# Residual sums of two MLPs run on in PSUM by ScalarE's copies; one product moves to another bank; squares are written in the transposes' order; the transposing transfers are issued on ScalarE's queue

## The chip, the cores and the metric

One core of a Trainium2 chip. TensorE (PE) multiplies, VectorE (DVE) and ScalarE (ACT) work elementwise, GpSimd (POOL) does little here, and SyncE (SP) issues DMA transfers; ACT can issue them too. Each engine works through its own list of instructions in order. The metric is the time of one execution in microseconds of the device.

## The reference

A trunk of two layers over 256 frames of width 2048, all in fp32. Each layer normalizes, mixes (layer 0 by stick-breaking attention, layer 1 by a top-64 sparse attention), adds to the residual `x`, and then runs an MLP, which is where this change lies:

```python
for i in range(DEPTH):                      # DEPTH = 2
    h = rms_norm(x, norm_mix[i])
    x = x + mixer(h)                        # one of two kinds
    h = rms_norm(x, norm_mlp[i])
    x = x + jnp.square(jax.nn.relu(h @ w_up[i])) @ w_down[i]   # 2048 -> 8192 -> 2048
```

## The kernel before

**Products.** An fp32 product is made of parts. Each weight tile is copied by ACT to a rounded first half `wh` (`copy`, L104), DVE subtracts to get the second half `wl` (L1002), and TensorE multiplies: the left operand's two parts with `wh`, its first part with `wl`. An item is one such weight tile: 12 matmuls of 128x512 for a tile of `w_down`, 6 for a tile of the products below. The function `load` (L968) issues the weight loads on SP's queue, `high` makes `wh` four items ahead, `low` makes `wl` three items ahead. There are five buffers for `wh` and four for `wl`.

**Blocks.** The MLP's hidden width of 8192 is worked in eight blocks f of 1024. Block 0 goes the plain way. Blocks 1 to 7 compute their part of `h @ w_up` by seven products of half the size instead of eight (`seven`), with sums of weights (`two`, `other`, `three`, `last_sum`: L406, L410, L415, L418) and sums of results. The first 16 items of a block accumulate P1 and another product in the two banks of one PSUM tile (`pair`, named acc) and two products in single banks (`v`, `z`, named aux). After them `between` copies P1 from the pair into SBUF (`se(0)`) and `between2` and later `after` and `after2` form the sums on DVE (L445 to L456). The last 12 items use the bank `y` for P2 and the pair again. `after` adds P1 and P2 on DVE (L451).

**From results to the hidden tile.** `square_up` applies Relu and Square on ACT. For blocks 1 to 6 the result must be turned so that tokens lie along the free axis: DVE transposes 32x32 pieces (`squares`, L473, reading 16 bytes apart), SP writes each half n of the tile to DRAM (`away`, L482, tile hd) and reads it back in another order (`back`, four transfers per half, L488); ACT and DVE then split it into the two parts of the hidden tile hS (`parted_h`, L494 and L495). Half 1 goes first, half 0 a little later. Block 7 is turned on TensorE (`turn`).

**Down.** `down(f)` multiplies hS with `w_down` in four groups of 512 columns, four items each, half 1 of hS first. A group accumulates in one of three PSUM tiles of two banks (acc). At its end `down_done` has DVE compute `xs = acc * rs2 + xs` for both token halves (L262; L532 for the last block of the last layer, in pieces of 256 columns, followed by the output transfers). `rs2` undoes the normalization, which is put off to here.

**Order.** The items of block f's products are spread among the down items of blocks f-2 and f-1, 28 + 16 items per block. The steps after the products are hung behind items by times in units of TensorE's work (`ends`, `LAPS`). Within these rules a scheduler that belongs to the build sets the order on each engine, except where an instruction is kept in program order (the loads, the transfers to and from DRAM, the splitting into hS).

Of the kernel before, what the change touches and what calls it, by code (L numbers as in the profile page):

```python
# [52 lines left out]
LAG = 2.7  # L53
RAWS = {"wraw": RAW, "sraw": 5}
# [11 lines left out]
class Item:  # L66


    def __init__(self, raws, a, b, mm, moving=False, source=None):
        self.raws, self.a, self.b, self.mm, self.moving, self.post = raws, a, b, mm, moving, []  # L70
        self.source, self.then, self.us = source or (lambda: raws[0].ap), None, 2.72

# [6 lines left out]
def trunk(ctx, tc, x, norm_mix, w_in_a, w_out_a, w_in_b, w_out_b, q_norm_b, k_norm_b, rel_bias,  # L79
# [126 lines left out]
    def tokens_out(items, key, w, r0, c0, lhs, q, done, n=KT, apart=False):  # L206


        def mm(wh, wl):
            if q == 0 and apart:  # L210
                accs[key] = [auxp.tile([P, 512], F32, name="aux") for _ in range(2)]
            elif q == 0:
                acc = accp.tile([P, 2, 512], F32, name="acc")
                accs[key] = [acc[:, t, :] for t in range(2)]
            acc = accs[key]
            for w, parts in ((wh, (0, 1)), (wl, (0,))):
                for t in range(2):
                    for j in range(KB):
                        k = KB * q + j
                        for part in parts:  # L220
                            pin(pe.matmul(acc[t], lhs(k, part, slice(t * P, (t + 1) * P)), w[:, j, :],  # L221
                                          start=w is wh and part == 0 and k == 0,
                                          stop=w is wl and k == n - 1))
        it = plain(rows(w, r0 + KB * P * q, KB * P, c0, 512), KB, 512, mm, True)
        if q == n // KB - 1:
            it.post.append(lambda: done(accs.pop(key)))
# [29 lines left out]
    def add_residual(c, next_col, acc, scale=None):  # L256
        for t in range(2):
            xc = xs[:, t, c * 512:(c + 1) * 512]
            if scale is None:
                dve.tensor_add(xc, acc[t], xc)  # L260
            else:
                dve.scalar_tensor_tensor(xc, acc[t], scale[:, t:t + 1], xc,  # L262
                                         op0=OP.mult, op1=OP.add)
# [15 lines left out]
    def mlp(l, next_col):  # L279
# [6 lines left out]
        def stats():  # L286
# [5 lines left out]
            dve.tensor_mul(sec["rs2"], sec["rs2"], sec["rs2"])  # L292

# [68 lines left out]
        def seven(f, c0):  # L362
# [38 lines left out]
            for s in range(HK // KB):  # L401
# [24 lines left out]
                second += [item([b21], single("y"), quarter(1, 0), s, lambda b=b21: b.ap),  # L426
# [21 lines left out]
            def after():  # L448
                g["s2"] = flat("jc")
                copy(g["s2"], pair(0)())  # L450
                dve.tensor_add(se(0), g["y"], se(0))  # L451
                dve.tensor_sub(se(2), se(2), pair(0)())

            def after2():
                dve.tensor_sub(se(1), se(1), pair(0)())
                dve.tensor_add(g["s2"], pair(1)(), g["s2"])  # L456

            def turn(n, c0, c1):
# [3 lines left out]
                for k in range(4):  # L462
                    for t, c in enumerate((c0, c1)):
                        pe.transpose(ps[:, k, t * P:(t + 1) * P], c[:, k * P:(k + 1) * P], ident)
# [4 lines left out]
            def squares(n, *cs):  # L469

                sq = g["sq", n]
                for t, c in enumerate(cs):
# [600 lines left out]
```

## Time and profile before

| | |
|---|---|
| time, median of 3 runs | 2113.52 us (2111.05 to 2117.68) |
| profiled execution, time and span | 2116.24 us, 2114.5 us |
| granted clock, mean | 0.994 |
| busy: PE, DVE, ACT | 2058.0, 1750.2, 1217.4 us |
| MLP of layer 0 and of layer 1, roughly | 399 to 1103 us, 1415 us to the end |
| residual sums L262: count, each | 120, 0.745 us |
| transposes L473: count, each | 48, 1.07 us |
| ACT's split into hS L494: count, idle before | 24, 39.2 us |

A group row names line, engine, operation, out<-in with shapes and count, then busy us and mean ns of one, then the idle time of the engine just before, and what ended it. In a timeline row the first numbers are the start and the length in us, and the bracket is the idle time before it with the instruction that ended it. SPq and ACTq are the DMA-issuing queues of SP and ACT. The profiled execution stands 2.7 us above the median of the runs shown.

### The profile page before, as it was taken

Reading aid. Unit: us, or ns where it says so; the run is one execution under the profiler, and the core shown is the slowest. Engines: PE = TensorE matmul, PEld = TensorE weight load, DVE = VectorE, ACT = ScalarE, POOL = GpSimd, SP = SyncE. Lnnn points to the kernel's source line nnn. Section 1 sums busy time; section 2 is a strip of 40 time slices with the busy share of each in tenths; the row PEclk is TensorE's granted clock in tenths of the full one; section 3 lists DMA queues with packets and bytes.
Section 4 is the critical chain, followed back from the end, with each engine's and each line's share of the span. In section 5 each row is a group of like instructions: output and inputs, shape, how many; then the busy total and the mean of one; then the engine's idle time right before and its main releaser. Section 6 shows DMA issues by size and latency. Waiting matters only on the chain.

```text
span 2114.5 us, 26501 instructions
## 1 busy us (share of the span) xinstructions
PE 2058.0 (97%) x9572; PEld 1697.1 (80%) x9572; DVE 1750.2 (83%) x1881; ACT 1217.4 (58%) x1560; POOL 34.1 (2%) x71
## 2 busy tenths in 40 slices
PE   8999999999999999999999999999999999999999
PEld 7888888888777787777888788888877778777787
DVE  5456665799999999999865877779999999999985
ACT  6445555665565655665654555666656556555562
POOL 0101110000000000000000000000000000000000
PEclk9999999999999999999999999999999999999999
DMA  7666645755766757677466565465585776757754
GB/s 257 192 184 191 181 161 179 227 191 198 230 203 211 230 192 239 201 226 223 167 195 191 156 195 174 150 208 182 198 258 172 227 228 200 248 189 236 209 180 142
DMA packets 274040, 424.04 MB, mean 201 GB/s; under 512 B 16498, under 2 KB 107252, under 8 KB 273908
## 3 DMA queue, kind: packets, MB, share of 16 engines
q1 hardware_dynamic: 266148, 414.92, 61.6%
q10 hardware_dynamic: 7760, 7.43, 1.2%
q8 instruction: 75, 1.23, 0.2%
q14 instruction: 57, 0.47, 0.1%
HBM read 404.41 MB, written 17.82 MB: 200 GB/s over the span
## 4 chain that ended last, share of the span: by engine, by line
PE 84%; DVE 8%; DMA 4%; SPq 2%; ACT 1%; issue 1%; DVEq 0%; ACTq 0%
PE acc L221 45%; PE acc L242 15%; PE acc L379 12%; PE aux L379 8%; DVE wl L1002 3%; DMA t<-hd 3%; DVE t L473 2%; SPq L488 1%; DVE wraw L406 1%; ACT wh L104 1%; PE aux L160 1%; DVE xs L262 1%; ACT hS L494 1%; DVE sraw L410 1%; PE aux L871 0%
## 5 line engine op out<-in xcount | busy, mean ns | idle before, releaser
L1002 DVE TENSOR_TENSOR wl<-wraw,wh 128x1024 fp32r<-128x1024 f32 x626 | 758.5, 1220 | 224.9 <-PE acc L221 112.0
L104 ACT ACTIVATE wh<-wraw 128x1024 fp32r<-128x1024 f32 x626 | 649.1, 1055 | 455.4 <-PE acc L221 171.2
L221 PE MATMUL acc<-wh,hS 128*128 128x512 f32 x2016 | 516.6, 391 | 23.4 <-ACT hS L494 22.8
L221 PEld LDWEIGHTS acc<-wh,hS 128*128 128x128 f32 x2016 | 377.3, 188 | 108.7 <-ACT hS L494 27.9
L104 ACT ACTIVATE wh<-sraw 128x1024 fp32r<-128x1024 f32 x224 | 233.8, 1055 | 205.4 <-DVE sraw L418 158.0
L1002 DVE TENSOR_TENSOR wl<-sraw,wh 128x1024 fp32r<-128x1024 f32 x224 | 270.7, 1219 | 22.4 <-PE acc L379 11.8
L221 PE MATMUL acc<-wl,hS 128*128 128x512 f32 x1008 | 269.7, 391 | 6.9 <-DVE wl L1002 6.9
L242 PE MATMUL acc<-xT,wh 128*128 128x512 f32 x896 | 230.4, 396 | 0.0
L221 PEld LDWEIGHTS acc<-wl,hS 128*128 128x128 f32 x1008 | 188.3, 188 | 50.4 <-DVE wl L1002 12.0
L242 PEld LDWEIGHTS acc<-xT,wh 128*128 128x128 f32 x896 | 159.8, 188 | 30.1
L221 PE MATMUL acc<-wh,xT 128*128 128x512 f32 x640 | 165.2, 397 | 0.5 <-ACT wh L104 0.5
L379 PE MATMUL aux<-wh,xS 128*128 128x512 f32 x448 | 128.7, 406 | 14.4 <-ACT wh L104 14.4
L221 PEld LDWEIGHTS acc<-wh,xT 128*128 128x128 f32 x640 | 119.6, 190 | 27.5 <-issue 2.3
L221 PE MATMUL acc<-wh,oT 128*128 128x512 f32 x512 | 133.1, 395 | 0.0
L242 PEld LDWEIGHTS acc<-xT,wl 128*128 128x128 f32 x896 | 122.1, 188 | 10.4
L242 PE MATMUL acc<-xT,wl 128*128 128x256 f32 x896 | 126.9, 281 | 0.0
L379 PE MATMUL acc<-wh,xS 128*128 128x512 f32 x448 | 126.1, 397 | 0.6
L379 PE MATMUL acc<-wh,xT 128*128 128x512 f32 x448 | 123.6, 398 | 0.0
L379 PEld LDWEIGHTS aux<-wh,xS 128*128 128x128 f32 x448 | 86.5, 196 | 38.3 <-ACT wh L104 20.4
L221 PEld LDWEIGHTS acc<-wh,oT 128*128 128x128 f32 x512 | 94.7, 188 | 18.9
L379 PEld LDWEIGHTS acc<-wh,xS 128*128 128x128 f32 x448 | 85.0, 192 | 21.9 <-ACT wh L104 4.5
L379 PEld LDWEIGHTS acc<-wh,xT 128*128 128x128 f32 x448 | 86.1, 192 | 18.3
(196 smaller groups left out, 2255.9 us busy)
## 6 DMA issues: line engine op xcount, KB each, us to landing
wraw<-in_w_down_dram SPq DMA_DIRECT2D x256, 512.0 KB, 4.7
sraw<-in_w_up_dram SPq DMA_DIRECT2D x168, 512.0 KB, 4.7
wraw<-in_w_in_a_dram SPq DMA_DIRECT2D x96, 512.0 KB, 3.7
wraw<-in_w_up_dram SPq DMA_DIRECT2D x88, 512.0 KB, 4.1
wraw<-in_w_in_b_dram SPq DMA_DIRECT2D x64, 512.0 KB, 3.7
wraw<-in_w_out_a_dram SPq DMA_DIRECT2D x32, 512.0 KB, 3.5
wraw<-in_w_out_b_dram SPq DMA_DIRECT2D x32, 512.0 KB, 4.0
hd<-t SPq DMA_DIRECT2D x24, 512.0 KB, 6.6
```

The costliest lines, as they stand in the source:

```text
L104: pin(act.activation(o, i, AF.Copy, scale=scale))
L160: pin(pe.transpose(ps[:, j, t * P:(t + 1) * P], block[t][:, ks], ident))
L221: pin(pe.matmul(acc[t], lhs(k, part, slice(t * P, (t + 1) * P)), w[:, j, :], start=w is wh and part == 0 and k == 0, stop=w is wl and k == ...
L242: pe.matmul(acc[:, m, cs], w[:, j, m * P:(m + 1) * P], xT[:, k, xs_, :], start=w is wh and k == 0, stop=w is wl and k == KT - 1)
L262: dve.scalar_tensor_tensor(xc, acc[t], scale[:, t:t + 1], xc, op0=OP.mult, op1=OP.add)
L379: pe.matmul(acc, x(k, part), w[:, j, :], start=opens and w is wh and part == 0 and k == 0, stop=w is wl and k == HK - 1, **on)
L406: dve.tensor_add(b11.ap, b11.ap, b12.ap)
L410: dve.tensor_add(b12.ap, b12.ap, b22.ap)
L473: dve.transpose(sq[:, t].rearrange("p (q k a) -> p q k a", q=4, k=4), c.rearrange("p (q b k) -> p q k b", q=4, k=4))
L488: tc.keep_in_program_order(nc.sync.dma_start(to[32 * q:32 * q + 32], hd[q]))
L494: tc.keep_in_program_order(act.activation(hi, raw, AF.Copy))
L1002: pin(dve.tensor_sub(wl, raw, wh.bitcast(F32)))
```

## The change

**Residual sums.** A down group's PSUM tile is opened six items ahead (`SEED`), and ACT copies the residual `xs` into it (`seeded`; in block 0 multiplied by 1/rs2, which `stats` now also computes). The matmuls of the group all accumulate. At the group's end ACT copies the tile back to `xs` (`down_done`); in the last block ACT and DVE each multiply one token half by rs2 on the way.

**P1 to P2's bank.** `between` copies P1 from the pair into the bank `y`, and P2's matmuls accumulate on top. `after` has ACT apply Relu from that bank; L451 goes.

**Squares and transposes.** `squared` has ACT write the squares in the order in which the transposes read them, into the tile that is later read back; the transposes (`turned`) then read and write without gaps, back into `se`.

**Transfers.** `away` and `back` are issued on ACT's queue, `away` as two transfers of 256 KB per half instead of one of 512 KB. The output transfers of the last block are shared between the queues by token half.

```diff
-    def tokens_out(items, key, w, r0, c0, lhs, q, done, n=KT, apart=False):
+    def tokens_out(items, key, w, r0, c0, lhs, q, done, n=KT, apart=False, seed=None):
+        def opened():
...
+            if seed:
+                seed(accs[key])
...
-                                          start=w is wh and part == 0 and k == 0,
-                                          stop=w is wl and k == n - 1))
+                                          start=not seed and w is wh and part == 0 and k == 0,
+                                          stop=w is wl and k == n - 1, skip_group_check=bool(seed)))
...
             def between():
-                copy(se(0), pair(0)())
                 g["s5"] = flat("jc")
                 copy(g["s5"], g["z"])
+                copy(single("y")(), pair(0)())
...
-                dve.tensor_add(se(0), g["y"], se(0))
+                act.activation(se(0), g["y"], AF.Relu)
...
+            def squared(n):
+                c0, c1 = (se(2), se(1)) if n else (se(0), g["s2"])
+                if n:
+                    act.activation(c0, c0, AF.Relu)
+                act.activation(c1, c1, AF.Relu)
+                for t, c in enumerate((c0, c1)):
+                    o = c if f == LASTF else g["sq", n][:, t].rearrange("p (q k b) -> p q b k", q=4, k=4)
+                    i = c if f == LASTF else c.rearrange("p (q b k) -> p q b k", q=4, k=4)
+                    act.activation(o, i, AF.Square)
...
-            def squares(n, *cs):
-                sq = g["sq", n]
-                for t, c in enumerate(cs):
-                    dve.transpose(sq[:, t].rearrange("p (q k a) -> p q k a", q=4, k=4),
-                                  c.rearrange("p (q b k) -> p q k b", q=4, k=4))
+            def turned(n):
+                for t, c in enumerate((se(2), se(1)) if n else (se(0), g["s2"])):
+                    dve.transpose(c, g["sq", n][:, t])
...
-                tc.keep_in_program_order(nc.sync.dma_start(hd.rearrange("t p c -> p t c"), g["sq", n]))
+                for t, c in enumerate((se(2), se(1)) if n else (se(0), g["s2"])):
+                    tc.keep_in_program_order(nc.scalar.dma_start(hd[t], c))
...
-                    tc.keep_in_program_order(nc.sync.dma_start(to[32 * q:32 * q + 32], hd[q]))
+                    tc.keep_in_program_order(nc.scalar.dma_start(to[32 * q:32 * q + 32], hd[q]))
...
+        def seeded(f, g, acc):
+            for t in range(2):
+                copy(acc[t], xs[:, t, 512 * g:512 * g + 512], scale=1.0 if f else sec["1/rs2"][:, t:t + 1])
         def down_done(f, g, acc):
-            if f < LASTF or next_col is not None:
-                add_residual(g, next_col if f == LASTF else None, acc, sec["rs2"])
-                return
...
+            if f < LASTF:
+                for t in range(2):
+                    copy(xc[t], acc[t])
+            elif next_col is not None:
+                copy(xc[0], acc[0], scale=by[0])
+                dve.tensor_scalar_mul(xc[1], acc[1], by[1])
+                prep(g, next_col)
...
+        if i + SEED < len(items) and items[i + SEED].before:
+            items[i + SEED].before()
         it.mm(*parts.pop(i))
```

Three places show what stands in a row on an engine. First, **DVE between the pair's sums and the next sum of weights**, before (block 2 of layer 0; se and jc are the block's results, L262 the residual sum):

```order
L456 TENSOR_TENSOR jc<-acc,jc 128x512
L1002 TENSOR_TENSOR wl<-wraw,wh 128x1024
L1002 TENSOR_TENSOR wl<-sraw,wh 128x1024
L1002 TENSOR_TENSOR wl<-wraw,wh 128x1024
L262 SCALAR_TENSOR_TENSOR xs<-acc,rs_3666,xs 128x512 x2
L1002 TENSOR_TENSOR wl<-wraw,wh 128x1024
L473 STREAM_TRANSPOSE t_5061<-se 128x512
L473 STREAM_TRANSPOSE t_5062<-se 128x512
L473 STREAM_TRANSPOSE t_5061<-se 128x512
L1002 TENSOR_TENSOR wl<-sraw,wh 128x1024
L473 STREAM_TRANSPOSE t_5062<-jc 128x512
L1002 TENSOR_TENSOR wl<-wraw,wh 128x1024
```

and now (L413, L417, L422 are the old L406, L410, L415; L1031 the old L1002):

```order
L463 TENSOR_TENSOR jc<-acc,jc 128x512
L417 TENSOR_TENSOR sraw<-sraw 128x1024
L422 TENSOR_TENSOR t_5097<-wraw,sraw 128x1024
L1031 TENSOR_TENSOR wl<-wraw,wh 128x1024
L492 STREAM_TRANSPOSE se<-t_5081 128x512
L492 STREAM_TRANSPOSE se<-t_5082 128x512
L492 STREAM_TRANSPOSE se<-t_5081 128x512
L1031 TENSOR_TENSOR wl<-sraw,wh 128x1024
L1031 TENSOR_TENSOR wl<-wraw,wh 128x1024 x2
L492 STREAM_TRANSPOSE jc<-t_5082 128x512
L1031 TENSOR_TENSOR wl<-sraw,wh 128x1024
L1031 TENSOR_TENSOR wl<-wraw,wh 128x1024
```

The two residual sums are gone; L417 and L422 come after the results' sums here, where their old counterparts came before. The next row in both is the next sum, L406 or L413.

Second, **SP from the first write of half 1 to the read-backs**, before (block 2 of layer 0):

```order
L482 DMA hd<-t_5061 128x2x512
L968 DMA wraw<-in_w_down_dram 128x2x512
L968 DMA sraw<-in_w_up_dram 128x2x512
L968 DMA wraw<-in_w_up_dram 128x2x512
L968 DMA sraw<-in_w_up_dram 128x2x512
L968 DMA wraw<-in_w_down_dram 128x2x512
L482 DMA hd<-t_5062 128x2x512
L488 DMA t_5061<-hd 32x8x128 x4
L968 DMA wraw<-in_w_down_dram 128x2x512
L488 DMA t_5062<-hd 32x8x128 x4
```

Now SP has only the loads. Third, **ACT from the write of half 0 to the hidden tile**, now (block 2 of layer 0; L106 is the old L104; L501 and L507 the old L482 and L488, L513 the old L494):

```order
L501 DMA hd<-se 128x512
L501 DMA hd<-jc 128x512
L106 ACTIVATE wh<-wraw 128x1024
L106 ACTIVATE wh<-sraw 128x1024
L507 DMA t_5081<-hd 32x8x128 x4
L507 DMA t_5082<-hd 32x8x128 x4
L106 ACTIVATE wh<-wraw 128x1024 x2
L106 ACTIVATE wh<-sraw 128x1024
L106 ACTIVATE wh<-wraw 128x1024
L106 ACTIVATE xs<-acc 128x512 x2
L106 ACTIVATE wh<-wraw 128x1024
L513 ACTIVATE hS<-t_5081 128x4x256
```

Both read-backs now stand together, in front of the copies `wh` that TensorE uses next. Ahead of the rows shown stand the write of half 1 and two more copies; before, ACT had no transfer here and only the copies and the split into hS.

More of the change, by code (lines that the diff above doesn't have):

```diff
@@ L53 @@
 LAG = 2.7
+SEED = 6
 RAWS = {"wraw": RAW, "sraw": 5}
@@ L71, in __init__ @@
         self.source, self.then, self.us = source or (lambda: raws[0].ap), None, 2.72
+        self.before = None
 def plain(src, a, b, mm, moving=False):
@@ L204, in rows, with mm @@
         return w[r0:r0 + nr, c0:c0 + ncol].rearrange("(a p) c -> p a c", p=P)
-    def tokens_out(items, key, w, r0, c0, lhs, q, done, n=KT, apart=False):
-        def mm(wh, wl):
-            if q == 0 and apart:
+    def tokens_out(items, key, w, r0, c0, lhs, q, done, n=KT, apart=False, seed=None):
+        def opened():
+            if apart:
                 accs[key] = [auxp.tile([P, 512], F32, name="aux") for _ in range(2)]
-            elif q == 0:
+            else:
                 acc = accp.tile([P, 2, 512], F32, name="acc")
                 accs[key] = [acc[:, t, :] for t in range(2)]
+            if seed:
+                seed(accs[key])
+        def mm(wh, wl):
+            if q == 0 and not seed:
+                opened()
             acc = accs[key]
@@ L254, in joined, with add_residual @@
         return u
-    def add_residual(c, next_col, acc, scale=None):
+    def add_residual(c, next_col, acc):
         for t in range(2):
             xc = xs[:, t, c * 512:(c + 1) * 512]
[L259 to L263, printed above, removed]
+            dve.tensor_add(xc, acc[t], xc)
         if next_col is not None:
@@ L292, in stats @@
             dve.tensor_mul(sec["rs2"], sec["rs2"], sec["rs2"])
+            sec["1/rs2"] = tmp.tile([P, 2], F32, name="rs3")
+            dve.reciprocal(sec["1/rs2"], sec["rs2"])
         def temp(name="t2", bufs=4):
@@ L463, in turn @@
                     for t, c in enumerate((c0, c1)):
-                        pe.transpose(ps[:, k, t * P:(t + 1) * P], c[:, k * P:(k + 1) * P], ident)
+                        pe.matmul(ps[:, k, t * P:(t + 1) * P], c[:, k * P:(k + 1) * P], ident,
+                                  start=k % 2 == 0 and t == 0, stop=k % 2 == 1 and t == 1, is_transpose=True,
+                                  skip_group_check=True)
                 hi = h[:, kts, 0, :]
@@ L495, in parted_h @@
                 tc.keep_in_program_order(dve.tensor_sub(lo, raw, hi.bitcast(F32)))
-            ends = [(0, after), (1.4, after2), (1.4, lambda: (square_up(se(2)), square_up(se(1)))),
-                    (2.8, lambda: (square_up(se(0)), square_up(g["s2"])))]
+            ends = [(0, after), (1.4, after2), (1.4, lambda: squared(1)), (2.8, lambda: squared(0))]
             if f == LASTF:
@@ L502, in seven @@
                 ends.append((0, homes))
-                for n, cs in ((1, lambda: (se(2), se(1))), (0, lambda: (se(0), g["s2"]))):
-                    steps = (lambda n=n, cs=cs: squares(n, *cs()), lambda n=n: away(n), lambda n=n: back(n),
-                             lambda n=n: parted_h(n))
+                for n in (1, 0):
+                    steps = (lambda n=n: turned(n), lambda n=n: away(n), lambda n=n: back(n), lambda n=n: parted_h(n))
                     ends += [(us + (0 if n else LAG), step) for us, step in zip(LAPS, steps)]
@@ L517, in down @@
                                lambda acc, g=g: down_done(f, g, acc), HK,
-                               apart=next_col is None and (f, g) == (LASTF, 3))
+                               apart=next_col is None and (f, g) == (LASTF, 3),
+                               seed=lambda acc, g=g: seeded(f, g, acc))
                     if f not in (0, LASTF):
```

19 lines of the change are left out of this document (12 added, 7 removed).

## Prediction, made before the change was run

> **What bounds the kernel now.** I read the page first (shares by engine), then the chain of waits for the pace of the blocks, then one block in the groups of DVE and ACT, and last the timeline of that block.
>
> ```profile
> PE 2058.0 (97%) x9572; PEld 1697.1 (80%) x9572; DVE 1750.2 (83%) x1881; ACT 1217.4 (58%) x1560; POOL 34.1 (2%) x71
> ```
>
> TensorE is busy 97% of the span, which looks as if nothing were left. The share is an average, and a matmul's modelled end hides short gaps. So I take the chain, where the four transposes of a block (L473) recur once per block:
>
> ```profile
> 525.44 2.07 DVE t L473 x2
> 964.41 2.02 DVE t L473 x2
> 1540.92 2.04 DVE t L473 x2
> 1974.74 2.02 DVE t L473 x2
> 2064.00 35.38 PE acc L221 x156
> ```
>
> From 525.44 to 964.41 lie five blocks: 87.8 us each. From 1540.92 to 1974.74 five more: 86.8 us. Mean 87.3. A matmul that waits for nothing takes 35.38/156 = 0.2268 us. One block, measured:
>
> ```profile
> 585.00:673.50 88.50, 84.05 (x360) 68.01 (x359) 83.70 (x81) 51.58 (x57) 0.00 (x0) 0.98 0.67 212
> L1002 DVE TENSOR_TENSOR wl<-wraw,wh 128x1024 fp32r<-128x1024 f32 x24 | 29.0, 1218 | 1.9 <-ACT wh L104 1.0 <-PE acc L221 0.8
> L262 DVE SCALAR_TENSOR_TENSOR xs<-acc,rs,xs 128x512 f32<-128x512 f32 x8 | 5.6, 744 | 0.0
> L473 DVE STREAM_TRANSPOSE t<-se 128x512 f32<-128x512 f32 x3 | 3.0, 1053 | 0.0
> L473 DVE STREAM_TRANSPOSE t<-jc 128x512 f32<-128x512 f32 x1 | 1.1, 1079 | 0.0
> L451 DVE TENSOR_TENSOR se<-aux,se 128x512 f32<-128x512 f32 x1 | 0.7, 684 | 0.0
> L104 ACT ACTIVATE jc<-acc 128x512 f32<-128x512 f32 x1 | 0.6, 600 | 0.7 <-PE acc L379 0.7
> ```
>
> (Columns of the first row: the stretch, its length, busy us and count of PE, PEld, DVE, ACT, POOL, then clock, DMA share, GB/s.) 360 matmuls at 0.2268 are 81.6 us, so a mean block loses 87.3 - 81.6 = 5.7 us. DVE has 83.70 us of work in it, more than TensorE's 81.6: with DVE's order, not TensorE's, the block ends. Where it shows:
>
> ```profile
> 600.71 0.60 ACT L104 ACTIVATE jc<-acc 128x512 f32<-128x512 f32 x1 [0.70 <-PE acc L379]
> 615.04 0.37 SPq L482 DMA_DIRECT2D hd<-t  x1
> 618.15 1.21 DVE L406 TENSOR_TENSOR wraw<-wraw,sraw 128x1024 f32<-128x1024 f32 x1
> 618.28 1.19 PE L221 MATMUL acc<-wl,hS 128*128 128x512 f32 x4 [0.61 <-DVE wl L1002]
> 619.46 1.06 ACT L104 ACTIVATE wh<-wraw 128x1024 fp32r<-128x1024 f32 x1 [8.07 <-DVE wraw L406]
> 620.57 1.20 PE L379 MATMUL aux<-wh,xS 128*128 128x512 f32 x4 [1.09 <-ACT wh L104]
> 625.19 0.37 SPq L968 DMA_DIRECT2D wraw<-in_w_down_dram  x1
> 626.18 3.88 SPq L488 DMA_DIRECT2D t<-hd  x4
> 632.90 1.93 SPq L488 DMA_DIRECT2D t<-hd  x4
> 635.97 1.06 ACT L494 ACTIVATE hS<-t 128x1024 fp32r<-128x1024 f32 x1 [1.29 <-DMA t<-hd]
> 637.08 0.50 PE L221 MATMUL acc<-wh,hS 128*128 128x512 f32 x1 [2.68 <-ACT hS L494]
> 637.42 0.98 PE L379 MATMUL acc<-wl,xS 128*128 128x512 f32 x2
> 641.29 0.63 PE L379 MATMUL acc<-wl,xT 128*128 128x512 f32 x2
> ```
>
> Count from 600.7, when the pair's last matmul has ended and its copy starts. DVE finishes the next sum of weights (L406) at 619.4, 18.7 us on; ACT idles 8.07 us for it, and TensorE then waits 0.61 and 1.09 us. SP, held behind loads until 625.19, issues the read-back at 626.18. The hidden tile hS is there at 637.03, 36.3 us on, and TensorE waits 2.68 us. After that it runs slow: 10 matmuls from 637.42 to 641.29 take 3.87 us instead of 2.27, 1.6 us lost, where the block's granted clock is 0.98. So the hS wait costs about 4.3 us of that block's 6.9 (88.5 - 81.6), DVE's late sums and halves most of the rest. Over the kernel:
>
> ```profile
> PE acc L221 <- ACT hS L494: 22.8, 12, 2.7
> PE aux L379 <- ACT wh L104: 14.4, 14, 1.1
> PE acc L221 <- DVE wl L1002: 6.9, 12, 0.6
> ```
>
> Twelve waits for hS (six blocks in each of two layers), and 14 waits of 1.03 us for a first-half copy, one in every block, the two last blocks too.
>
> **The change part by part.**
>
> *DVE.* The eight L262 (5.6 us) and L451 (0.7 us) go: 83.7 - 6.3 = 77.4 us per block. The four transposes stay, but read and write in order. Nothing before shows such a transpose; the bounds are today's 1.053 us and the 0.684 us of L451, the same 128x512 once through, so 0 to 1.5 us less. I count half. DVE comes to 76 to 77.4 us, under TensorE's 81.6: the bound passes to TensorE, if ACT lets it.
>
> The Trainium skill, page "SBUF — State Buffer", section "Door 1: The DMA port swizzle", says that an access which moves to a new 16-byte line each time pays a penalty, and the old transposes read elements 16 bytes apart. By that rule the whole 1.5 us goes here, and a part of it comes back in ScalarE's squares, which now write 128 bytes apart; no run here shows the latter.
>
> *ACT.* Added per block: eight seeds and eight drains of 128x512. A copy out of PSUM takes 0.600 us (row above); a copy into PSUM isn't shown, and I give it the same (bounds: the 0.52 us at which copies of this size follow each other, shown below, and 1.06, a copy of double length). 16 x 0.6 = 9.6 us. The copy of P1 and the four Relu and four Square stay in number; if a strided Square took as long as a strided transpose (1.05), that is 4 x 0.43 = 1.7 us more. The transfers:
>
> ```profile
> L710 ACTq DMA_DIRECT2D bv_d<-bv x4: 366/370/407, 138.0 to 216.0; - x4
> L818 ACTq DMA_DIRECT2D bias<-bv_d x8: 361/470/1413, 1102.7 to 1296.0; - x8
> DMA to landing us min/median/max: 2.7/6.6/8.5
> t<-hd SPq DMA_DIRECT2D x96, 128.0 KB, 6.1
> bias<-bv_d ACTq DMA_DIRECT2D x4, 256.0 KB, 4.3
> ```
>
> (The third row is that of today's writes to hd, from issue to landing.) Twelve issues per block at 0.37 to 0.47 are 4.4 to 5.6 us. ACT: 51.6 + 9.6 + 5 + 1 = about 67 of 81.6 us. Its sum fits. What counts is where it stands still.
>
> *The walk of one block after the change*, from the pair's last matmul; needs are matmuls counted in the built order times 0.2268. First use of hS comes after 150 matmuls, 34.0 us; before it was 137, 31.1 us. So the order alone gives 2.9 us more cover than before. Between the pair and the next block of sums DVE has the same rows in both orders, less two L262 (1.4 us, 5.6/8 each) and up to 1.5 by the transposes: the sum is there at 16 to 17.5 us instead of 18.7, its copy a microsecond later, needed after 84 matmuls, 19.0 us. I leave 0.3 of the 1.03 us wait. ACT issues the write only after two copies that wait for such sums: at 17 to 20 us (14.3 before, 615.04 - 600.7). It lands in 2.7 us when the engines are free (the minimum above; today's first write of a block). The read-back can be issued when the write has landed and two more pairs of copies are through: at 21 to 26 us, 23 taken (25.5 before, held by SP). Behind the read-back of the first half stands that of the second; in the built program each transfer shares a semaphore with the eighth before it, and so the last two wait until the first half's first two have landed. Until then ACT issues nothing: no first-half copies, drains or seeds. With 0.9 us of issuing and a landing between 4.3 us (ACT's own 256 KB loads of bias) and the 7.1 to 7.4 us of today's first half, ACT is free at 28 to 31; I take 28.5, near the small end, since the read-back no longer lies behind the loads in SP's queue.
>
> ```profile
> DMA to landing us min/median/max: 6.8/7.1/7.4
> 607.30 0.62 ACT L341 ACTIVATE se<-se 128x512 f32<-128x512 f32 x1
> 607.82 0.62 ACT L340 ACTIVATE jc<-jc 128x512 f32<-128x512 f32 x1
> 621.69 2.94 ACT L104 ACTIVATE wh<-wraw 128x1024 fp32r<-128x1024 f32 x3
> ```
>
> (The first row is that of the four read-backs at 626.18.) The next first half that ACT then owes is used after 132 matmuls, 29.9 us; the copy at 29.5 is just in time. Between the free ACT and hS stand five such copies (0.98 each in a row) and two drains (0.52 from start to start): 5.9 us, and 1.06 for hS: 35.5, needed at 34.0: 1.5 us of waiting, short enough that I put only 0.3 on the clock instead of 1.6. With 0.3 for late sums and 0.3 for restarts a block loses 2.4 instead of 5.7.
>
> The Trainium skill, page "DMA: Bandwidth & Descriptors", section "Issuing engines are not separate DMA queues", speaks against this part: all queues end on the same 16 DMA engines, so issuing from another engine saves only issue time. By it the landing stays at 7.1 us (rival 1).
>
> *Loads.* SP loses 10 issues per block and no longer stands in front of its loads for 3.88 + 1.93 us; the loads were issued behind DVE's releases anyway, so I count nothing; without that cover a load is late by what a landing is, 4.7 us, once.
>
> *The seeds* are issued six items ahead of their group, some 11 us of TensorE's work (6 x 81.6/44), against 1.2 us for the two: hidden. In the last block of each layer drains go half to ACT, half to DVE. The end:
>
> ```profile
> 2109.84 1.66 DVE L532 SCALAR_TENSOR_TENSOR xs<-aux,rs,xs 128x256 f32<-128x256 f32 x4 [7.64 <-PE aux L221]
> ```
>
> Four in a row become two beside two: about 0.7 us off the end.
>
> *Sum.* 12 blocks x (5.7 - 2.4) = 39.6; the two last blocks get most of a 1.03 us wait and its restart back, 2 x 1.2 = 2.4; the end 0.7. Together 43 us. The profiled execution took 2116.24 us (span 2114.5 and 1.7 around it), so 2073; it lies 2.7 over the median of 2113.52, so I forecast **2070 us**. Its own range, a block's loss between 1.4 and 3.5, is 2057 to 2084.
>
> **The rivals.**
>
> 1. *The transfers are no quicker on ACT.* For it: the first half's read-back, issued when loads filled the engines, took 7.1 us. Against: today it lies behind those loads in one queue. ACT is free at 23 + 0.9 + 7.1 = 31.0, the copy at 32.0 is 2.1 late, hS at 38.0 against 34.0 + 2.1: 1.9. With 0.8 for clock, sums and restarts a block loses 4.8, 0.9 saved: 12 x 0.9 + 3 = 14, **2100 us**.
> 2. *ACT becomes the bound, slower.* ACT reaches the read-back at 26 (each copy in front runs to its end first) and stands until 26 + 0.9 + 7.1 = 34.0. The copy at 35.0 is 5.1 late, hS at 41.0 against 39.1: 1.9; after such a wait the clock costs 1.6 again, sums 0.4: 9.0 a block against 5.7: 12 x 3.3 - 3 = 37 us more, **2150**; half of that, 2131, if it happens in every other block. It decides from a free ACT at about 32 us on.
> 3. *All is covered.* Transposes at 0.68, landing at 4.3, read-back at 21: ACT free at 27, hS at 34.0: a block loses 0.5: 12 x 5.2 + 3 = 65, **2048 us**.
> 4. *Nothing happens*: TensorE waits as long as today, only for ACT: **2113 us**. For it, today's wait ends with ACT's hS, not with DVE; against it, the 13 matmuls more of cover.
>
> **How the numbers follow.** Forecast 0.50, rival 1 0.15, rival 2 0.13, rival 3 0.15, rival 4 0.07. A change of under 0.3% (6.3 us) can't be told from none here. Faster by more: 0.50 + 0.15 + 0.15 = 0.80; within: 0.07; slower: 0.13. The range goes from 2044 (rival 3 and a little beyond) to 2112, where rival 2 and part of rival 4 are left out.
>
> **What would show it.** Right: the waits of TensorE for hS fall from 22.8 us in all to under 15 and its waits for a first half from 14.4 to under 6, DVE's busy time in a block is 75 to 78 us, ACT's 62 to 70, blocks follow at 83 to 85.5 us, the granted clock of the blocks returns to 1.0, and ACT shows one standstill per block, ended by the read-back. Wrong: TensorE's longest total wait is for a first half behind an ACT that waits for a DMA; or a Square takes over 1 us and the transposes wait for it; or blocks stay at 87 us with an idle DVE.

## The result, and the profile after

The changed kernel takes **2138.32 us** (median of 4 runs, 2134.07 to 2141.32) against 2115.6 us (2111.05 to 2119.97) for the kernel before beside it: a ratio of **1.0106, 95% interval 1.0077 to 1.0135**. It is 22.7 us slower, where 2070 us and a range of 2044 to 2112 were forecast. The profiled execution took 2137.75 us, its span 2136.0.

First the waits of the changed kernel (engine, line and tile, what they waited for; us in all, times, longest):

```profile
ACT wh L106 <- DMA t<-hd: 87.4, 11, 9.2
...
PE aux L386 <- ACT wh L106: 21.7, 21, 2.9
...
PE acc L228 <- DVE hS L514: 4.1, 12, 0.3
PE acc L386 <- DVE wl L1031: 3.9, 9, 0.4
```

The wait for ACT's hS, 22.8 us before, no longer stands in the list (under 15 was forecast). That isn't because hS comes early: in block 2 of layer 0 it is there 37.1 us after the pair's copy starts, against 36.3 before (36.4 to 39.2 over the twelve blocks, against 34.9 to 36.6). TensorE has been held up ahead of it: the wait for first halves rose from 14.4 to 21.7 us, behind an ACT that stands 87.4 us for read-backs. Yet these waits of TensorE together are no longer than before (29.7 against 22.8 + 14.4 + 6.9 = 44.1), so they alone can't make a slower kernel. The stretches show what can. Blocks 2 to 5 of each layer (columns as in the prediction):

```profile
610.53:962.13 351.60, 342.02 (x1442) 268.75 (x1441) 311.78 (x286) 246.76 (x293) 0.00 (x0) 1.00 0.68 216
1631.69:1986.66 354.97, 344.38 (x1442) 272.54 (x1441) 311.81 (x286) 246.87 (x293) 0.00 (x0) 0.99 0.68 213
```

DVE is down to 77.9 us per block, ACT up to 61.7. But **TensorE itself is busy 342 to 344 us** for the 1442 matmuls, 85.5 to 86.1 us per block, at a granted clock of 1.00 and 0.99. The kernel before, same four blocks of each layer:

```profile
612.00:963.41 351.41, 335.82 (x1442) 272.40 (x1441) 335.97 (x321) 205.64 (x228) 0.00 (x0) 0.99 0.68 216
1625.71:1973.74 348.03, 333.38 (x1442) 269.68 (x1441) 335.53 (x321) 205.31 (x228) 0.00 (x0) 1.00 0.68 218
```

A block takes 87.9 and 88.7 us now, 87.9 and 87.0 before, and TensorE was busy 335.82 and 333.38 us for the four. These eight blocks hold only 7.1 of the 21.5 us by which the span grew; the rest lies outside them. Over the whole span TensorE is busy 2092.9 us instead of 2058.0, and idle 43.1 instead of 56.5: its work got longer, not its waits. Where nothing waits and the change touches nothing, in the output projection of layer 0, the timeline of the kernel before reads

```profile
368.06 1.98 PE L221 MATMUL acc<-wh,oT 128*128 128x512 f32 x8
369.87 1.07 PE L221 MATMUL acc<-wl,oT 128*128 128x512 f32 x4
370.78 1.98 PE L221 MATMUL acc<-wh,oT 128*128 128x512 f32 x8
```

and that of the changed kernel

```profile
369.77 2.03 PE L228 MATMUL acc<-wh,oT 128*128 128x512 f32 x8
371.63 1.09 PE L228 MATMUL acc<-wl,oT 128*128 128x512 f32 x4
372.57 2.03 PE L228 MATMUL acc<-wh,oT 128*128 128x512 f32 x8
```

Twelve matmuls took 370.78 - 368.06 = 2.72 us, now 372.57 - 369.77 = 2.80: **0.2333 us from start to start instead of 0.2267**, 2.9% more. The largest group over the whole kernel (busy us, then the mean ns of one), before and now:

```profile
L221 PE MATMUL acc<-wh,hS 128*128 128x512 f32 x2016 | 516.6, 391 | 23.4 <-ACT hS L494 22.8 <-DVE hS L495 0.5
```

```profile
L228 PE MATMUL acc<-wh,hS 128*128 128x512 f32 x2016 | 526.1, 397 | 5.5 <-DVE hS L514 4.1 <-ACT hS L106 0.5
```

The groups wl,hS, wh,oT and wl,oT rose by 4 to 5 ns, wl,xS, which has waits beside it, by 9 and 16; the products of the layer input, wh,xT (L228), did not (398 ns against 397).

The second finding is the standstill, in block 2 of layer 0 of the changed kernel (timeline; the pair's sums start at 603.25):

```profile
603.25 0.60 ACT L106 ACTIVATE jc<-acc 128x512 f32<-128x512 f32 x1 [0.79 <-PE acc L386]
621.45 0.83 ACTq L501 DMA_DIRECT2D hd<-se  x2
624.43 1.04 ACTq L507 DMA_DIRECT2D t<-hd  x2
625.50 7.98 ACTq L507 DMA_DIRECT2D t<-hd  x6
633.60 2.02 ACT L106 ACTIVATE wh<-wraw 128x1024 fp32r<-128x1024 f32 x2 [7.30 <-PE acc L228]
634.71 1.20 PE L386 MATMUL aux<-wh,xS 128*128 128x512 f32 x4 [0.75 <-ACT wh L106]
```

ACT issues the write 18.2 us after the pair, the read-back 21.2 us after, and stands in the last six transfers until 633.48. (The bracket names PE as the last releaser by the profile, but it had long been done; what ended it were the landings: in the built program the last two of the eight wait for the first two.) TensorE waits for the next first half. Over the twelve blocks ACT is free 29.5 to 32.3 us after the pair's copy starts, 30.9 in the mean.

### The profile page after: what moved, and what is told of

The parts are those of the page before. It is cut to its first block, busy times and chain, and to the rows that moved or that the text cites. A ratio compares the mean times of both kernels' runs of the same rounds, so it can differ in the third digit from the quotient of the medians.

```text
span 2136.0 us, 26611 instructions
## 1 busy us (share of the span) xinstructions
PE 2092.9 (98%) x9572; PEld 1692.6 (79%) x9572; DVE 1662.4 (78%) x1745; ACT 1371.6 (64%) x1812; POOL 34.3 (2%) x71
## 4 chain that ended last, share of the span: by engine, by line
PE 82%; DMA 7%; DVE 4%; ACT 3%; issue 3%; ACTq 0%; DVEq 0%; SPq 0%
PE acc L228 46%; PE acc L251 15%; PE acc L386 10%; PE aux L386 7%; DMA t<-hd 5%; DVE wl L1031 2%; ACT wh L106 2%; DMA wraw<-in_w_down_dram 1%; ACT t L474 1%; DVE wraw L413 1%; DVE hS L514 1%; PE aux L162 1%; DMA hd<-se 1%; PE aux L228 1%; PE aux L900 0%
## 5 line engine op out<-in xcount | busy, mean ns | idle before, releaser
L1031 DVE TENSOR_TENSOR wl<-wraw,wh 128x1024 fp32r<-128x1024 f32 x626 | 758.6, 1221 | 331.5 <-PE acc L228 155.1
L106 ACT ACTIVATE wh<-wraw 128x1024 fp32r<-128x1024 f32 x626 | 654.7, 1058 | 464.4 <-PE acc L228 170.9
L228 PE MATMUL acc<-wh,hS 128*128 128x512 f32 x2016 | 526.1, 397 | 5.5 <-DVE hS L514 4.1
L228 PEld LDWEIGHTS acc<-wh,hS 128*128 128x128 f32 x2016 | 377.1, 188 | 104.9 <-DVE hS L514 9.3
L1031 DVE TENSOR_TENSOR wl<-sraw,wh 128x1024 fp32r<-128x1024 f32 x224 | 272.4, 1221 | 31.7 <-PE acc L386 16.0
L106 ACT ACTIVATE wh<-sraw 128x1024 fp32r<-128x1024 f32 x224 | 235.0, 1055 | 79.6 <-DVE sraw L425 53.6
L228 PE MATMUL acc<-wl,hS 128*128 128x512 f32 x1008 | 274.0, 395 | 0.0
L228 PEld LDWEIGHTS acc<-wl,hS 128*128 128x128 f32 x1008 | 189.4, 188 | 45.6
L251 PEld LDWEIGHTS acc<-xT,wh 128*128 128x128 f32 x896 | 159.7, 188 | 30.2
L228 PE MATMUL acc<-wh,xT 128*128 128x512 f32 x640 | 165.4, 398 | 0.5 <-ACT wh L106 0.5
L386 PE MATMUL aux<-wh,xS 128*128 128x512 f32 x448 | 126.0, 402 | 21.8 <-ACT wh L106 21.7
L228 PEld LDWEIGHTS acc<-wh,xT 128*128 128x128 f32 x640 | 119.9, 190 | 27.7 <-issue 2.3
L228 PE MATMUL acc<-wh,oT 128*128 128x512 f32 x512 | 135.6, 400 | 0.0
L386 PE MATMUL acc<-wh,xS 128*128 128x512 f32 x448 | 126.0, 404 | 0.0
L386 PE MATMUL acc<-wh,xT 128*128 128x512 f32 x448 | 122.1, 394 | 0.0
L386 PEld LDWEIGHTS aux<-wh,xS 128*128 128x128 f32 x448 | 82.3, 188 | 49.0 <-ACT wh L106 31.3
L228 PEld LDWEIGHTS acc<-wh,oT 128*128 128x128 f32 x512 | 94.7, 188 | 21.3
L386 PEld LDWEIGHTS acc<-wh,xS 128*128 128x128 f32 x448 | 84.9, 192 | 22.7 <-ACT wh L106 3.6
L386 PEld LDWEIGHTS acc<-wh,xT 128*128 128x128 f32 x448 | 84.5, 189 | 19.7
```

What stands on the lines that cost most here:

```text
L106: pin(act.activation(o, i, AF.Copy, scale=scale))
L251: pe.matmul(acc[:, m, cs], w[:, j, m * P:(m + 1) * P], xT[:, k, xs_, :], start=w is wh and k == 0, stop=w is wl and k == KT - 1)
L386: pe.matmul(acc, x(k, part), w[:, j, :], start=opens and w is wh and part == 0 and k == 0, stop=w is wl and k == HK - 1, **on)
L1031: pin(dve.tensor_sub(wl, raw, wh.bitcast(F32)))
```

## The experiments

The kernel before, run beside these, had medians of 2113.92, 2116.52 and 2113.52 us in the three groups. Ratios are to it.

| kernel | us | ratio, 95% interval |
|---|---|---|
| after_at_old_addresses | 2113.92 | 0.9998 (0.9982 to 1.0014) |
| before_64_bytes_on | 2145.67 | 1.0154 (1.0121 to 1.0186) |
| before_transfers_on_act | 2135.37 | 1.0103 (1.0072 to 1.0134) |
| old_addresses_transfers_on_sp | 2067.30 | 0.9782 (0.9753 to 0.9810) |
| sp_128_bytes_on | 2089.19 | 0.9875 (0.9852 to 0.9899) |
| sp_32_bytes_on | 2093.71 | 0.9897 (0.9874 to 0.9920) |
| sp_64_both | 2075.89 | 0.9812 (0.9789 to 0.9836) |
| sp_old_turns | 2084.14 | 0.9856 (0.9836 to 0.9875) |
| back0_on_sp | 2077.14 | 0.9828 (0.9810 to 0.9847) |
| sp_sums_only | 2085.20 | 0.9861 (0.9845 to 0.9877) |
| pool_transfers | 2053.48 | 0.9715 (0.9696 to 0.9733) |
| sp_512_bytes_on | 2067.91 | 0.9780 (0.9758 to 0.9802) |

### The pace of TensorE: addresses, or the work beside it?

`stats` got a new tile for 1/rs2. It is 8 bytes wide, and with two buffers, each rounded up to 32 bytes, it takes 64 bytes of the pool `tmp`. Everything allocated behind it moved; the weight buffers and xT did not. Byte addresses within a partition, from the two built programs:

```
                         before   after
xT                        18432   18432
wh, streamed part         72192   72192   (and every 4608 on)
xS                       119808  119872
oT (layer 0)             138752  138816
hS                       173056  173120
```

All those of before are multiples of 512; after, xS, oT and hS are 64 off.

**The changed kernel at the old addresses:**

```diff
-            sec["rs2"] = tmp.tile([P, 2], F32, name="rs2")
+            both = tmp.tile([P, 4], F32, name="rs2")
+            sec["rs2"], sec["1/rs2"] = both[:, 0:2], both[:, 2:4]
...
-            sec["1/rs2"] = tmp.tile([P, 2], F32, name="rs3")
```

> The changed kernel, except that 1/rs2 lies in the second half of rs2's tile instead of a tile of its own. The new tile had moved every tile allocated behind it (hS, oT, xS, the temporaries) on by 64 bytes; here they lie where they lay before the change, and the instructions are those of the changed kernel. Theory 1 (addresses): matmuls whose left operand lies in a moved tile follow each other at 0.2333 us in the changed kernel and at 0.2268 before; here they return to 0.2268, the groups wh,hS / wl,hS / wh,oT / wl,oT / wl,xS lose about 24 us together, and the time is about 2112 (2102 to 2118). Theory 2 (the slower pace comes from the work that runs beside TensorE: seeds, drains or strided squares): the pace stays at 0.2333 and the time at 2138.

Measured: 2113.92 us, level with the kernel before, 24.4 us under the changed kernel. Its largest group, where the changed kernel has 526.1 us and 397 ns:

```profile
L228 PE MATMUL acc<-wh,hS 128*128 128x512 f32 x2016 | 514.0, 391 | 5.2 <-DVE hS L514 3.8 <-ACT hS L106 0.8
```

**The kernel before with the tile:**

```diff
             sec["rs2"] = tmp.tile([P, 2], F32, name="rs2")
+            sec["1/rs2"] = tmp.tile([P, 2], F32, name="rs3")
+            dve.reciprocal(sec["1/rs2"], rs)
```

> The kernel before, with only the 8-byte tile (and the one small reciprocal per layer that fills it) added, nothing else of the change. Its section tiles lie at the addresses of the changed kernel. Theory 1 (addresses): pace 0.2333 for matmuls on hS and oT, about 24 us slower than before, 2140 (2130 to 2146). Theory 2 (the work beside): the pace stays 0.2268 and the time 2115.

Measured: 2145.67 us, 31.8 us over the kernel before. Its group and its waits:

```profile
L221 PE MATMUL acc<-wh,hS 128*128 128x512 f32 x2016 | 529.3, 396 | 25.4 <-ACT hS L496 25.2 <-DVE hS L497 0.2
```

```profile
PE acc L221 <- ACT hS L496: 25.2, 12, 3.0
PE aux L381 <- ACT wh L104: 14.1, 14, 1.1
```

The waits are nearly those of before (22.8 and 14.4); what changed is the pace. Both runs agree with theory 1, and theory 2 falls: at the old addresses the pace is 391 ns with all the seeds, drains and squares beside it, and without them it is 396 at the moved ones. 64 bytes cost 24 to 32 us, which is as much as the whole result.

### ScalarE's queue

**Before, with only the transfers moved:**

```diff
-                tc.keep_in_program_order(nc.sync.dma_start(hd.rearrange("t p c -> p t c"), g["sq", n]))
+                tc.keep_in_program_order(nc.scalar.dma_start(hd.rearrange("t p c -> p t c"), g["sq", n]))
...
-                    tc.keep_in_program_order(nc.sync.dma_start(to[32 * q:32 * q + 32], hd[q]))
+                    tc.keep_in_program_order(nc.scalar.dma_start(to[32 * q:32 * q + 32], hd[q]))
```

> The kernel before, with only the two transposing transfers (to hd and back) issued on ScalarE's queue instead of SyncE's; all else and all addresses as before. If ScalarE's standstill behind the read-back costs (the prediction's rival 2): ScalarE shows one wait of about 8 us per block before a copy wh, TensorE's wait for a first half rises from 14.4 us in all to over 20, and the time is 8 to 20 us over before, about 2128. If the transfers are quicker there, as forecast: hS earlier, its wait of 22.8 us under 10, time 2100. If neither: 2115.

Measured: 2135.37 us, 21.5 us slower. Its waits:

```profile
PE aux L379 <- ACT wh L104: 30.0, 25, 2.9
PE acc L221 <- ACT hS L494: 17.0, 11, 1.7
```

That is a little more than the 8 to 20 us expected. The first halves are late (30.0 against 14.4 us). hS is not earlier: in block 2 of layer 0 it is there 36.8 us after the pair's copy starts, against 36.3 before. TensorE waits less for it (17.0 against 22.8), since the first halves have already held it up. The profile puts only three of ACT's waits down to a read-back (23.4 us), though the read-backs take 7.7 to 10.0 us from their first issue to their last in every block.

**The changed kernel at the old addresses, transfers on SP:** `nc.scalar` becomes `nc.sync` in `away` and `back`.

> The changed kernel at the old addresses, with the transposing transfers back on SyncE's queue (still two writes per half). If ScalarE's standstill behind the read-back is what ate the forecast's gain: TensorE's wait for a first half falls from 21.7 us to under 8, the standstill of 87 us in all before copies wh is gone, and the time is 10 to 20 us below that of the changed kernel at the old addresses, about 2097. If the standstill is covered anyway: the same time as that kernel within 5 us. If SyncE holds the read-back behind its loads, a wait for hS comes back (over 10 us) and the two cancel.

Measured: **2067.30 us** (2067.22 to 2067.66), 46.6 us under the same kernel with ACT's queue and 2.2% under the kernel before; only 10 to 20 us were expected. hS is there 34.0 to 34.2 us after the pair's copy starts. Its waits and two of its stretches of four blocks:

```profile
PE aux L386 <- ACT wh L106: 5.3, 12, 0.4
...
PE acc L228 <- DVE hS L514: 2.5, 11, 0.2
```

```profile
601.73:934.93 333.20, 330.28 (x1442) 269.15 (x1441) 310.69 (x286) 246.29 (x293) 0.00 (x0) 1.00 0.72 227
1590.49:1923.59 333.10, 330.20 (x1442) 269.16 (x1441) 310.80 (x285) 246.22 (x293) 0.00 (x0) 1.00 0.72 227
```

With ACT's queue, at the same addresses:

```profile
604.21:949.73 345.52, 335.80 (x1442) 270.47 (x1441) 311.23 (x286) 246.51 (x293) 0.00 (x0) 0.99 0.69 219
1611.94:1962.80 350.86, 336.30 (x1442) 271.71 (x1441) 311.23 (x286) 246.68 (x293) 0.00 (x0) 0.99 0.68 216
```

A block takes 83.3 us instead of 86.4 and 87.7. Of the 12.3 us between the first rows of the two, TensorE's busy time has 5.5 and its idle time 6.8. I read the 5.5 as the price of restarts after waits (the granted clock is 0.99 against 1.00): nearly as much as the waits.

**Only the read-back of half 0 on SP:**

```diff
-                    tc.keep_in_program_order(nc.scalar.dma_start(to[32 * q:32 * q + 32], hd[q]))
+                    tc.keep_in_program_order((nc.scalar if n else nc.sync).dma_start(to[32 * q:32 * q + 32], hd[q]))
```

> The changed kernel at the old addresses (2113.9 us), with only the read-back of half 0, the last four transfers of a block, moved from ScalarE's queue to SyncE's; the writes and the read-back of half 1 stay on ScalarE. In the changed kernel ScalarE stands in the last two of these four until the first two of half 1 have landed, about 7.4 us. If that is what the transfers on ScalarE cost: no standstill ended by a read-back, TensorE's waits for a first half fall from 26.1 us to under 8, and the time is 2067 to 2075. If issuing any transfer there costs (the writes, the first four): 2085 to 2105.

Measured: 2077.14 us, 36.8 us of the 46.6 regained, 2 us above the range expected. No copy wh of ACT waits for a read-back any more. The timeline shows where the standstill went, and the waits what is left:

```profile
699.93 0.72 ACTq L507 DMA_DIRECT2D t<-hd  x1
700.68 2.40 ACTq L507 DMA_DIRECT2D t<-hd  x2
703.48 5.70 SPq L507 DMA_DIRECT2D t<-hd  x4
712.05 1.06 ACT L106 ACTIVATE wh<-wraw 128x1024 fp32r<-128x1024 f32 x1 [1.45 <-DMA wraw<-in_w_down_dram]
714.32 0.51 PE L228 MATMUL acc<-wh,hS 128*128 128x512 f32 x1 [1.82 <-ACT hS L513]
```

```profile
PE acc L228 <- ACT hS L513: 10.0, 10, 3.0
PE aux L386 <- ACT wh L106: 5.0, 12, 0.5
```

Now SP stands 5.70 us in these four, a load behind it is late, ACT waits 1.45 us for that load in front of hS, and TensorE 1.82 for hS. So the standstill belongs to the four transfers that wait for landings, not to issuing on ACT as such, and it costs what stands behind it in that queue: the 9.8 us that are left over SP's 2067.30 are about what TensorE now waits for hS, 10.0.

**All transfers on GpSimd's queue:** `nc.gpsimd` in `away` and `back`, at the old addresses.

> The changed kernel at the old addresses with the transposing transfers on GpSimd's queue, which is busy 34 us of the span and has nothing else to do in the MLPs. If an idle queue is better than SyncE's, where a read-back stands behind loads and a load behind a read-back: 2062 to 2067. If nothing is left to gain since TensorE is busy 99%: 2067. If a transfer issued there takes longer to land or occupies the engines that issue it: 2070 to 2090, with waits for hS.

Measured: **2053.48 us**, 2.85% under the kernel before, the best of all and below the 2062 expected at best. Its stretch of four blocks, the issues, and the wait for hS:

```profile
600.32:929.41 329.09, 327.86 (x1442) 270.00 (x1441) 307.33 (x285) 246.55 (x293) 27.60 (x48) 1.00 0.72 230
```

```profile
t<-hd POOLq DMA_DIRECT2D x96, 128.0 KB, 5.8
hd<-se POOLq DMA_DIRECT2D x36, 256.0 KB, 3.6
```

```profile
ACT hS L513 <- DMA t<-hd: 8.4, 10, 1.5
```

A block takes 82.3 us, 0.7 over TensorE's 81.6. GpSimd is busy 27.60/4 = 6.9 us per block with twelve transfers, and a read-back lands in 5.8 us (5.6 on SP's queue, 7.1 on ACT's at these addresses). hS is there 30.0 to 31.0 us after the pair's copy starts, 3 to 4 us sooner than with SP's queue. In an engine that nobody waits for, the standstill is free. How much of the 13.8 us under SP's queue comes from the earlier hS and how much from loads that no longer stand behind read-backs, no run here separates.

### The parts that gain

Both at the old addresses, with SP's queue.

**Old transposes.** Squares in place, transposes with the 16-byte step, and the write takes their result from the other tile, as before:

```diff
-                    act.activation(o, i, AF.Square)
+                    act.activation(c, c, AF.Square)
...
-                    dve.transpose(c, g["sq", n][:, t])
+                    dve.transpose(g["sq", n][:, t].rearrange("p (q k a) -> p q k a", q=4, k=4),
+                                  c.rearrange("p (q b k) -> p q k b", q=4, k=4))
```

> The changed kernel at the old addresses with the transfers on SyncE's queue (2067.3 us), with the squares written in place and the transposes reading 16 bytes apart as before the change. DVE gets 4 x 0.39 us more per block, ScalarE 4 x 0.56 us less. If the cheaper transposes carry part of the gain: 2072 to 2080. If DVE's relief by the residual sums is enough by itself: 2066 to 2069.

Measured: 2084.14 us, 16.8 us slower than with the new order (15.6 by the two ratios), more than the 5 to 13 expected. Its waits for first halves are 10.2 us in 24 pieces, against 5.3 in 12:

```profile
PE aux L386 <- ACT wh L106: 10.2, 24, 0.4
```

**Residual sums alone** (P1 through SBUF again, old squares and transposes):

```diff
+                copy(se(0), pair(0)())
...
-                copy(single("y")(), pair(0)())
...
-                act.activation(se(0), g["y"], AF.Relu)
+                dve.tensor_add(se(0), g["y"], se(0))
```

> Of the change only the residual sums by ScalarE (seeds and drains), with 1/rs2 in rs2's tile, and the write in two transfers per half; P1 goes through SBUF as before, squares and transposes are as before, transfers are on SyncE's queue. If the residual sums carry most of the 46.6 us between before (2113.9) and the changed kernel at the old addresses with SyncE's queue (2067.3): 2085 to 2092 (the strided transposes cost 17 us in the run before, P1 some more). If the sums alone gain little because the block then ends with another of DVE's rows: above 2100.

Measured: 2085.20 us, 1.39% or about 29 us under the kernel before. The ranges of this kernel and of the one with old transposes but P1 in PSUM overlap (2084.07 to 2085.30, 2083.39 to 2087.41): moving P1 shows no gain. So the sums bring about 29 us, the turn's order, put on top of them, about 17. The 29 are not the sums' alone: this run also writes each half in two transfers of 256 KB instead of one, and has the new end of the last block. What these bring by themselves wasn't timed.

### Which addresses collide

All four start from the kernel of 2067.30 us; a spare small tile moves xS, oT and hS on.

```diff
+            spare = tmp.tile([P, 2], F32, name="rs3", bufs=1)     # 32 bytes; [P, 10] x2: 128; [P, 64] x2: 512
+            dve.reciprocal(spare[:, 0:2], rs)
```

For `sp_64_both`, `[P, 2]` with two buffers, and the streamed weights moved within their buffers:

```diff
-SHIFT = 8
+SHIFT = 24
```

> The same, with the section tiles moved on by 32 bytes instead. If only a place on a multiple of 64 or 128 bytes is good: 2090 to 2098, like 64 bytes. If the weights' tiles and the section tiles collide only at a distance of 64: 2067.

> The changed kernel at the old addresses with the transfers on SyncE's queue (2067.3 us), and a spare small tile (with one small reciprocal per layer into it) that moves the section tiles hS, oT, xS on by 128 bytes. If what counts is the place within 128 bytes, the pace stays at 0.2268 and the time at 2067 to 2069. If any displacement against the tuned layout costs: 2090 or more.

> The same, with the section tiles moved on by 64 bytes, and the weights that stream through TensorE (the products whose left operand is hS, oT, xS or part of xT) moved on by 64 bytes within their buffers as well. If the distance between the two operands is what counts: hS, oT and xS at 0.2268, and now the products with xT, which has not moved, slow: wh,xT and wl,xT lose about 6.5 ns each, 960 to 1900 of them, 6 to 12 us, 2073 to 2080 in all. If the place of the left operand alone counts: hS, oT, xS at 0.2333, xT unchanged, 2092 to 2098. If the streamed operand's place counts too: all slow, above 2100.

> The changed kernel at the old addresses with the transfers on SyncE's queue (2067.3 us), with the section tiles moved on by 512 bytes by a larger spare tile. If the two operands collide by their distance within 512 bytes (a row of the left operand is 512 bytes): the pace is 0.2268 and the time 2067 to 2069. If any distance other than the tuned one is slower: 2088 or more.

Measured: 2093.71, 2089.19, 2075.89 and 2067.91 us. The same stretch of the output projection, moved on by 32 bytes:

```profile
368.21 2.03 PE L228 MATMUL acc<-wh,oT 128*128 128x512 f32 x8
370.08 1.09 PE L228 MATMUL acc<-wl,oT 128*128 128x512 f32 x4
```

by 128 bytes:

```profile
368.81 2.02 PE L228 MATMUL acc<-wh,oT 128*128 128x512 f32 x8
370.67 1.10 PE L228 MATMUL acc<-wl,oT 128*128 128x512 f32 x4
```

by 512 bytes:

```profile
368.51 1.98 PE L228 MATMUL acc<-wh,oT 128*128 128x512 f32 x8
370.33 1.07 PE L228 MATMUL acc<-wl,oT 128*128 128x512 f32 x4
```

both operands by 64 bytes:

```profile
368.06 1.98 PE L228 MATMUL acc<-wh,oT 128*128 128x512 f32 x8
369.87 1.07 PE L228 MATMUL acc<-wl,oT 128*128 128x512 f32 x4
```

A place on a multiple of 128 is not enough, and a place 64 off is good if both operands share it. So it is the **distance** between the left operand and the streamed weights that counts: with the left operand 0 and 512 bytes beyond the weights' place they run at full pace, with 32, 64 and 128 they don't (from the rows, (370.08 - 368.21)/8 = 0.234 us each at 32, 0.2325 at 128, 0.2275 at 512). That a distance of 512 counts as none rests on the one run. In the last kernel the products with xT, which has not moved, are the ones at a distance, 64 bytes the other way, and they lose a little: 392 ns against 389 (acc<-wh,xT, L388 there, L386 in the kernel of 2067.30). Those 2 to 3 ns are under half of what 64 bytes the first way cost, and the kernel stands 8.6 us over 2067.30. Why, stays open, as does a distance of 256, which wasn't tried.

## Why the prediction was wrong

It missed by 2138 - 2070 = 68 us. Two causes carry it: 24.4 us from the addresses (2138.32 - 2113.92), and 43.9 from 2113.92 down to the forecast, nearly what ACT's queue costs (46.6). That the kernel with SP's queue stands at 2067.30, close to 2070, is partly luck: the forecast reckoned with transfers on ACT's queue and with 2.4 us lost per block, where this kernel has them on SP's and loses 83.3 - 81.6 = 1.7. The range given for the forecast alone has a slip of its own: a loss of 1.4 gives 2113.5 - 12 x 4.3 - 3 = 2059, not 2057.

**Right: what bounds the kernel, and what relieves it.** DVE was to fall from 83.7 to 76 to 77.4 us per block; it is 77.9. ACT was to reach 67 with 5 us of issuing, which the busy time leaves out; it is 61.7 without. A copy into or out of PSUM was taken at 0.600 us. Groups of the changed kernel:

```profile
L106 ACT ACTIVATE acc<-xs 128x512 f32<-128x512 f32 x110 | 65.4, 595 | 0.9
L106 ACT ACTIVATE xs<-acc 128x512 f32<-128x512 f32 x112 | 61.0, 596 | 13.9 <-PE acc L228 13.9
L474 ACT ACTIVATE t<-se 128x512 f32<-128x512 f32 x36 | 39.8, 1179 | 0.0
L492 DVE STREAM_TRANSPOSE se<-t 128x512 f32<-128x512 f32 x36 | 22.7, 678 | 0.0
```

The bound does pass to TensorE: with SP's queue a block takes 83.3 us, where 84.0 was forecast and 83 to 85.5 named as the sign. "So the order alone gives 2.9 us more cover than before" fits the run with SP's queue: hS is there 34.1 us after the pair's copy starts, where 34.0 was the need, and TensorE waits 0.2 us in all for ACT's part of it. In the changed kernel it can't be seen, since hS came later than before and TensorE was held up ahead of it.

**Mis-sized, without harm: the transposes.** "I count half" of 1.5 us per block; 4 x (1.053 - 0.678) is 1.5 us, all of it. A strided Square takes 1.179 us, 0.56 more than the 0.62 of a plain one: 2.2 us for the four of a block, where the bound was 4 x 0.43 and 1 us stood in ACT's sum. The Trainium skill, page "SBUF — State Buffer", section "Door 1: The DMA port swizzle", ties a penalty to moving on to a new 16-byte line with each element; both rows agree with it, and by it the whole 1.5 us was to be had. Among the signs of failure stood "a Square takes over 1 us and the transposes wait for it". The first half came true; the second did not (no idle time stands before the transposes in their row). The order still gains 17 us; I read that as ACT having room (61.7 us a block) where DVE (77.9) had little.

**Failed, first step: what the change costs beside its parts.** The whole sum rests on "A matmul that waits for nothing takes 35.38/156 = 0.2268 us", carried over to the changed kernel, and the tile for 1/rs2 was counted as nothing. It moved hS, oT and xS by 64 bytes, and their matmuls took 0.2333 us. No rival had a place for this. Undoing it is worth 24.4 us, adding it to the kernel before costs 31.8 (interval of the ratio 1.0121 to 1.0186, so 26 to 39). In the changed kernel a slower TensorE hides part of ACT's standstill: its wait for first halves is 21.7 us with the moved addresses and 26.1 without. That may account for some of the difference between 24 and 32; it isn't much beyond the intervals.

**Failed, second step: the price of ACT's standstill.** The walk itself held in the block shown: the next sum of weights 16.8 us after the pair (16 to 17.5 forecast), write at 17 to 20 us after the pair (18.2), read-back between 21 and 26 (21.2, with 23 taken), ACT free between 28 and 31 (30.2, with 28.5 taken; in five of the twelve blocks it is past 31). By its early read-back ACT would have been free 1.8 us sooner than I said; but the last transfer was issued 9.1 us after the first, where I had counted 5.5 (28.5 - 23). "I take 28.5, near the small end, since the read-back no longer lies behind the loads in SP's queue" is the wrong choice. The read-backs land no sooner on ACT's queue:

```profile
t<-hd ACTq DMA_DIRECT2D x96, 128.0 KB, 7.4
```

It was 6.1 us before. The Trainium skill, page "DMA: Bandwidth & Descriptors", section "Issuing engines are not separate DMA queues", says that another issuing engine saves only issue time; this row agrees. The rows of the writes don't: hd<-se lands in 2.5 us from ACT's queue and in 5.1 from SP's, both at the old addresses. So the forecast was right about the write (2.7 us) and wrong about the read-back, and it is the read-back that ACT stands for. Rival 1 built on read-backs that are no quicker and had a chance of 0.15. Its landing was right, and its block (4.8 us lost, 2100 us) is nearest to what the blocks lose with ACT's queue at the old addresses: (86.4 + 87.7)/2 - 81.6 = 5.4 us, so it is still too cheap. The missing piece, as far as the rows show, is "I put only 0.3 on the clock instead of 1.6": TensorE's busy time shows 5.5 to 6.1 us per four blocks more than with SP's queue, 1.4 to 1.5 a block. Short waits are followed by slow matmuls as well, four in 1.20 us in the row of 634.71 instead of the 1.09 in the row of 371.63.

**The rivals.** Rival 2 (ACT the bound, slower) had the sign right but not the mechanism alone: without the 64 bytes the kernel is level with before. Rival 4 gave the time of that kernel, 2113, but for another reason than that nothing happens: a gain of 46.6 us by the sums and the turn's order and a loss of the same size by the queue cancel. Of the signs for failure, "TensorE's longest total wait is for a first half behind an ACT that waits for a DMA" is what the waits show.

## What to carry to other kernels

A change that allocates anything can move everything behind it: compare the addresses of matmul operands, and the start-to-start time of matmuls in a stretch that the change leaves alone, before looking at its parts. A transfer that must wait for another's landing belongs in the queue of an engine that nobody waits for; what it costs is what stands behind it in that queue, and of the kernels here the idle GpSimd's was best by 13.8 us over SyncE's and 60.4 over ScalarE's. Parts with opposite signs can add up to nothing, so time them apart at fixed addresses: here the sums (with the split write) gave about -29 us, the turn's order -17, the queue +47, the addresses +24.

## What the runs showed that was not expected

TensorE's pace for these fp32 matmuls depends on the distance between its two operands in SBUF, taken within 512 bytes as far as it was tried: about 0.2267 us from start to start at 0 and 512, about 0.2333 at 32, 64 and 128. The trace of the kernel before already had both paces, in products where the weights are the left operand and lie 32 bytes below a multiple of 512, with xT on a multiple:

```profile
112.17 2.03 PE L242 MATMUL acc<-xT,wh 128*128 128x512 f32 x8
```

2.03 us for eight, beside 1.98 for the others; that the distance is the cause there as well wasn't tried. And the queue of GpSimd, with twelve transfers per block in 6.9 us of its time, had its read-backs land about as soon as SyncE's (5.8 against 5.6 us) and its writes hd<-se sooner (3.6 against 5.1; 2.5 on ScalarE's queue).
